# Two layers of experts on one core: the u product as one lo matmul of 256 and one hi matmul of 512 columns, a second search over 64 candidates, and three smaller edits

## The chip, the cores and the metric

The kernel runs as one program on one core of a Trainium2 chip. The metric is the time of the whole program on the device, in microseconds, as the median of the runs.

## The reference, cut to what matters

Two blocks run one after the other on 256 tokens of width 1024. Each is a mixer (S5 in block 0, NSA attention in block 1), and behind it `peer`, a search over 16384 experts:

```python
def peer(h, w_q, sub_keys, u_tab, v_tab):
    qk = (h @ w_q).reshape(b, s, H, 2, PEER_HALF)            # H = 8 heads
    sc = jnp.einsum('bshcd,hckd->bshck', qk, sub_keys)       # 128 scores per half
    s1, i1 = lax.top_k(sc[..., 0, :], K)                     # K = 16
    s2, i2 = lax.top_k(sc[..., 1, :], K)
    cand = (s1[..., :, None] + s2[..., None, :]).reshape(b, s, H, K * K)
    cidx = (i1[..., :, None] * PEER_NKEYS + i2[..., None, :]).reshape(b, s, H, K * K)
    top_s, top_pos = lax.top_k(cand, K)
    experts = jnp.take_along_axis(cidx, top_pos, axis=-1)
    gates = jax.nn.softmax(top_s, axis=-1)
    ...
        act = jax.nn.gelu(jnp.einsum('cd,ced->ce', hc, u_tab[ec])) * gc
        return jnp.einsum('ce,ced->cd', act, v_tab[ec])
```

## The kernel before

The kernel doesn't gather experts. It computes all 16384 of them for all tokens. Transposed, `B[expert, token] = gelu(u · h)`, held as 128 units of 128 experts (`NJ` = 128); then the gates, scattered to all experts, are multiplied in, and `B` times v gives the output. One `peer_layer` has these stages.

**U** (`U`, L724): for each unit j, 128 x 1024 weights are loaded (`load_unit`, L126, SP queue, `RAW` = 6 buffers shared by every load of the kernel), split into `w_hi` (an ACT copy to the short form fp32r, L139) and `w_lo` (a DVE subtraction, L181), and multiplied with h, which is split the same way into `h_hi` and `h_lo`. `mm3` (L184) issues three matmuls of 256 columns for each of the 8 slices k of the width: w_hi·h_hi (L188), w_hi·h_lo (L189), w_lo·h_hi (L190). That makes 24 matmuls a unit. Two units share one PSUM bank of 512, and `evac` takes both at once: one ACT gelu, and for the tokens that already have gates one DVE product more (L738).

**Route** (`route_steps`, L846): q for each head, scores, `topk1` (16 of 128 by MAX8, FIND_INDEX8 and MATCH_REPLACE8), `topk2` (16 of 256 sums), and `decode` (L913), which turns positions into expert numbers.

**G** (`G`, L752): 64 steps of 4 tokens. Each step writes two one-hot tables of 1024 columns on DVE (`oij` L762, `ohl` L765), multiplies them in 8 matmuls of 128 columns (L770), and multiplies the 512 results into `B` on DVE (L773), as far as the units of U are done (`ugelu`); what isn't done yet gets a copy on ACT (L776). The pool of `oij` and `ohl` has two buffers each.

**VS** (`VS`, L789): for each j, the v unit is split like u, `B[:, j]` is split into `a_hi` (ACT) and `a_lo` (DVE), and 12 matmuls of 512 columns (L799) add to four banks `acc`. In layer 0 `ada_steps` (L219) runs beside it on DVE: one load of `ada_t` and one pass of 1024 columns (L233) per step, 56 steps; DVE and SP follow the written order here.

**What sets the order.** `weave` (L698) mixes the steps of U into route and then into G by planned costs: each step yields (PE us, DVE us), and another U unit is drawn while the planned DVE time is ahead of the planned PE time. A U unit yields 2.62 for PE and `U_DVE` = 1.3 for DVE (0.6 more for each second unit once gates exist); a G step yields 0.5 and 1.5. What is left of U is drawn in VS, one unit per j, and while it lasts `credit` for ada steps grows by 0.8 per j, after that by 0.4. `peer_end` (L817) copies the four banks out (ACT L827 and DVE L825), transposes them and adds to x.

In the NSA stage `scores` (L1148) computes, for each pair of heads, head `par` = 0 from rows 0 to 63 of `qT` and `kT`, then head 1 from rows 64 to 127: a matmul of 128 columns (L1155), one of 256 (L1157), and two masks (L1159, L1160). In S5, `copies` (L568) writes `u` with the tokens of a channel in chunk order, and the matmuls of L613 read it through a strided view.

Of the kernel before, what the change touches and what calls it, by code (L numbers as in the profile page):

```python
# [282 lines left out]
class Norm:  # L283


    def __init__(self, K, g, layer, part, rs, bufs=4):
# [1130 lines left out]
```

## Time and profile before

| what | value |
|---|---|
| times of three runs | 2096.7, 2101.8, 2094.01 us |
| median | 2096.7 us |
| the profiled execution: its time, its span | 2095.41 us, 2093.6 us |
| PE busy | 2036.0 us, 97% |
| DVE busy | 1611.3 us, 77% |
| ACT busy | 1154.3 us, 55% |

By the trace S5 ends near 200 us; layer 0 of peer has its route stage to 412, G to 655 and VS to 1047; NSA ends near 1237; layer 1 of peer has decode in 1350 to 1455, G to 1690 and VS to 2080. Busy time of an engine is a sum over instructions; matmuls overlap one another, so the pace of a run of matmuls is read from their starts, not from their lengths. Idle time of an engine counts only where it is the one that others wait for.

### The profile page before, as it was taken

The numbers are of one execution on the slowest core, as the hardware profiler recorded it, in microseconds if no ns is written. First come the engines' busy times: TensorE is split into PE (matmuls) and PEld (weight loads), VectorE is DVE, ScalarE is ACT, GpSimd is POOL, SyncE is SP. The second block draws the span as 40 slices with busy tenths as digits, with TensorE's granted clock in tenths as the row PEclk, the third lists the DMA queues.
The fourth block names the chain that finished last, engine by engine and source line by source line (L and its number), as shares of the span: only waits on it lengthen the run. The fifth ranks groups of instructions, "written<-read, shape, count | busy, mean of one in ns | idle before, by whom it ended". The sixth has DMA issues, their size and how long they took to land. (4 is left out here: it accounts for less than half of the span.)

```text
span 2093.6 us, 39285 instructions
## 1 busy us (share of the span) xinstructions
PE 2036.0 (97%) x14344; PEld 1842.8 (88%) x14344; DVE 1611.3 (77%) x3698; ACT 1154.3 (55%) x2396; POOL 113.3 (5%) x149
## 2 busy tenths in 40 slices
PE   6899999999999999999999999999999999999998
PEld 3789999899999988888888689999999998888887
DVE  8696899878887777777766769998788865566555
ACT  4775555554445555555545655555454455555554
POOL 4220001200000000000010000022000000000000
PEclk9899999999999999999999999999999999999999
DMA  7445555544446788888863035555444455666663
GB/s 282 149 180 162 162 173 172 160 151 135 140 140 190 260 271 274 267 269 272 270 221 101 21 129 165 172 171 162 141 132 142 141 177 184 194 193 196 193 192 100
DMA packets 102690, 377.18 MB, mean 180 GB/s; under 512 B 11488, under 2 KB 11872, under 8 KB 101472
## 3 DMA queue, kind: packets, MB, share of 16 engines
q1 hardware_dynamic: 101520, 371.42, 55.8%
q0 software_dynamic: 544, 2.61, 0.4%
q8 instruction: 112, 1.84, 0.3%
q14 instruction: 82, 0.67, 0.1%
q10 hardware_dynamic: 432, 0.65, 0.1%
HBM read 373.07 MB, written 1.05 MB: 179 GB/s over the span
## 5 line engine op out<-in xcount | busy, mean ns | idle before, releaser
L139 ACT ACTIVATE w_hi<-raw 128x512 fp32r<-128x512 f32 x1194 | 746.8, 628 | 737.8 <-PE bank L189 433.5
L181 DVE TENSOR_TENSOR w_lo<-raw,w_hi 128x512 fp32r<-128x512 f32 x1194 | 814.9, 704 | 132.5 <-ACT w_hi L139 130.2
L188 PE MATMUL bank<-h_hi,w_hi 128*128 128x256 f32 x2504 | 717.3, 289 | 9.0 <-ACT w_hi L139 5.6
L190 PE MATMUL bank<-h_hi,w_lo 128*128 128x256 f32 x2504 | 709.1, 286 | 10.7 <-DVE w_lo L181 10.7
L189 PE MATMUL bank<-h_lo,w_hi 128*128 128x256 f32 x2504 | 709.5, 284 | 1.4 <-DVE h_lo L304 1.4
L188 PEld LDWEIGHTS bank<-h_hi,w_hi 128*128 128x128 f32 x2504 | 485.2, 195 | 17.1 <-ACT w_hi L139 7.5
L190 PEld LDWEIGHTS bank<-h_hi,w_lo 128*128 128x128 f32 x2504 | 480.2, 193 | 15.3 <-DVE w_lo L181 14.7
L189 PEld LDWEIGHTS bank<-h_lo,w_hi 128*128 128x128 f32 x2504 | 483.1, 193 | 3.8 <-DVE h_lo L304 2.7
L799 PE MATMUL bank<-w_lo,a_hi 128*128 128x512 f32 x1024 | 399.0, 390 | 0.2 <-DVE w_lo L181 0.2
L799 PE MATMUL bank<-w_hi,a_lo 128*128 128x512 f32 x1024 | 398.5, 389 | 0.0
L799 PE MATMUL bank<-w_hi,a_hi 128*128 128x512 f32 x1024 | 281.0, 390 | 0.0
L181 DVE TENSOR_TENSOR a_lo<-B,a_hi 128x256 fp32r<-128x256 f32 x256 | 108.9, 425 | 197.9 <-ACT a_hi L139 197.8
L799 PEld LDWEIGHTS bank<-w_hi,a_lo 128*128 128x128 f32 x1024 | 192.3, 188 | 39.8
L799 PEld LDWEIGHTS bank<-w_lo,a_hi 128*128 128x128 f32 x1024 | 192.3, 188 | 39.8 <-DVE w_lo L181 0.7
L799 PEld LDWEIGHTS bank<-w_hi,a_hi 128*128 128x128 f32 x1024 | 191.5, 188 | 38.6
L770 PE MATMUL bank<-ohl,oij 128*128 128x128 f16 x1024 | 129.2, 307 | 0.0
L139 ACT ACTIVATE a_hi<-B 128x256 fp32r<-128x256 f32 x256 | 106.7, 418 | 27.0 <-PE bank L799 14.4
L773 DVE SCALAR_TENSOR_TENSOR B<-bank,B 128x216 f32<-128x216 f32 (+31 forms) x128 | 62.5, 488 | 71.9 <-PE bank L770 71.1
L770 PEld LDWEIGHTS <-oij 128*128 128x128 f16 x1024 | 101.5, 128 | 4.2
L762 DVE TENSOR_TENSOR oij<-iota,slotT 128x1024 f16<-128x1024 f16 x128 | 89.2, 698 | 0.0
L765 DVE TENSOR_TENSOR ohl<-oij,slotT 128x1024 f16<-128x1024 f16 x128 | 88.8, 695 | 0.1
L233 DVE SCALAR_TENSOR_TENSOR raw<-raw,cb 128x1024 f32<-128x1024 f32 x56 | 68.3, 1219 | 0.0
(263 smaller groups left out, 1790.2 us busy)
## 6 DMA issues: line engine op xcount, KB each, us to landing
raw<-peer_u SPq DMA_DIRECT2D x256, 512.0 KB, 3.6
raw<-peer_v SPq DMA_DIRECT2D x256, 512.0 KB, 4.3
raw<-ada_t SPq DMA_DIRECT2D x56, 512.0 KB, 4.6
raw<-ada_w SPq DMA_DIRECT2D x40, 512.0 KB, 5.4
raw<-w_q SPq DMA_DIRECT2D x32, 512.0 KB, 3.5
raw<-w_glu SPq DMA_DIRECT2D x16, 512.0 KB, 4.1
raw<-w_in SPq DMA_DIRECT2D x8, 512.0 KB, 6.3
w<-w_cmp SPq DMA_DIRECT2D x4, 1024.0 KB, 9.4
```

What stands on the lines that cost most here:

```text
L139: nc.scalar.activation(hi, raw, AF.Copy)
L181: K.nc.vector.tensor_tensor(lo, raw, hi.bitcast(F32), op=OP.subtract)
L188: nc.tensor.matmul(out, wh, xh, start=start, stop=False)
L189: nc.tensor.matmul(out, wh, xl, start=False, stop=False)
L190: nc.tensor.matmul(out, wl, xh, start=False, stop=stop)
L233: V.scalar_tensor_tensor(w, w, 1.0, cb, op0=OP.mult, op1=OP.mult, accum_out=part[:, m:m + 1])
L762: V.tensor_tensor(oij.rearrange("p a n j t -> p (a n) j t"), tab[:, None].to_broadcast(full), si, op=OP.is_equal)
L765: V.tensor_tensor(ohl, oj, slotT[:, 1, 2 * q:2 * q + 2, :, None, :].to_broadcast([P, 2, 2, P, 2]), op=OP.mult)
L770: nc.tensor.matmul(pv[:, :, t], oij[:, t // 2, 0, :, t % 2], ohl[:, t // 2, n, :, t % 2], start=(n == 0), stop=(n == 1), skip_group_check= ...
L773: V.scalar_tensor_tensor(B[:, :jd, ts], pv[:, :jd], 1.0 / GS, B[:, :jd, ts], op0=OP.mult, op1=OP.mult)
L799: nc.tensor.matmul(acc[t][dh], a[al][:, ts], w[wl], start=(j == 0 and al + wl == 0), stop=(j == NJ - 1 and al == 1))
```

## The change

1. **U product.** `h_hi` and `h_lo` become halves of one tile `h2`. For each k there are now two matmuls: w_lo·h_hi of 256 columns, which opens the accumulation in the left half of a bank, and w_hi·[h_hi, h_lo] of 512 columns over the whole bank. A unit has a bank of its own. `evac` runs for each unit: ACT copies the left half to `B`, DVE adds the right half, ACT takes the gelu in place; where gates exist, the same on a tile `ge`, and then the product. A unit now yields 2.5 and `U_DVE` = 1.65 (0.3 more once gates exist). `ROUTE_J` goes from 64 to 72.
2. **Second search.** `topk2` searches 64 of the 256 sums, those that can be among the best 16 (four adds build them), and `places` turns their positions back, once per layer; the weights' exponentials of both token halves move ahead of it.
3. **Scores by turns**: the two heads' matmuls alternate, each head with its own bank.
4. **u by steps**: S5 writes `u` in the order in which L613 reads it.

```diff
-        self.hi = K.hpool.tile([P, KC, S], F32R, name="h_hi")
-        self.lo = K.hpool.tile([P, KC, S], F32R, name="h_lo")
+        K.h2 = K.hpool.tile([P, KC, 2, S], F32R, name="h2")
+        self.hi, self.lo = K.h2[:, :, 0], K.h2[:, :, 1]
...
-        u = tp.tile([P, S], F32, name="u", bufs=3)
+        u = us[k] = tp.tile([P, L, S // L], F32, name="u", bufs=3)
...
-        nc.scalar.activation(u, ps, AF.Copy)
-        us[k] = u.rearrange("p (c s) -> p s c", s=L)
+        nc.scalar.activation(u, pv, AF.Copy)
...
             def evac():
-                c, ps = late.pop()
-                pv = ps.rearrange("p (j t) -> p j t", j=2)
+                j, ps = late.pop()
                 t0 = done[0]
-                out = B[:, 2 * c:2 * c + 2]
+                out = B[:, j]
                 if t0 < S:
-                    nc.scalar.activation(out[:, :, t0:], pv[:, :, t0:], AF.Gelu_apprx_tanh)
+                    nc.scalar.activation(out[:, t0:], ps[:, t0:S], AF.Copy)
+                    V.tensor_add(out[:, t0:], out[:, t0:], ps[:, S + t0:])
+                    nc.scalar.activation(out[:, t0:], out[:, t0:], AF.Gelu_apprx_tanh)
                 if t0 > 0:
-                    g = wp.tile([P, 2, S], F32, name="ge", bufs=1)
-                    nc.scalar.activation(g[:, :, :t0], pv[:, :, :t0], AF.Gelu_apprx_tanh)
-                    V.tensor_mul(out[:, :, :t0], g[:, :, :t0], out[:, :, :t0])
-                ugelu[0] = 2 * c + 2
-                return 0.6 if t0 else 0.0
-
-            for c in range(NJ // 2):
+                    g = wp.tile([P, S], F32, name="ge")
+                    nc.scalar.activation(g[:, :t0], ps[:, :t0], AF.Copy)
+                    V.tensor_add(g[:, :t0], g[:, :t0], ps[:, S:S + t0])
+                    nc.scalar.activation(g[:, :t0], g[:, :t0], AF.Gelu_apprx_tanh)
+                    V.tensor_mul(out[:, :t0], g[:, :t0], out[:, :t0])
+                ugelu[0] = j + 1
+                return 0.3 if t0 else 0.0
+
+            for j in range(NJ):
                 ps = bank(K)
-                for m in range(2):
-                    chunk_T(K, split_w(K, load_unit(K, u_src[layer, 2 * c + m])), h, ps[:, m * S:(m + 1) * S])
-                    dve = evac() if late and m == 0 else 0.0
-                    yield 2.62, U_DVE + dve
-                late.append((c, ps))
+                w = split_w(K, load_unit(K, u_src[layer, j]))
+                for k in range(KC):
+                    hi, lo = w[k // 4]
+                    cs = slice((k % 4) * P, (k % 4 + 1) * P)
+                    nc.tensor.matmul(ps[:, :S], lo[:, cs], h[0][:, k], start=(k == 0), stop=False, skip_group_check=True)
+                    nc.tensor.matmul(ps, hi[:, cs], K.h2[:, k].rearrange("p a t -> p (a t)"), start=False,
+                                     stop=(k == KC - 1), skip_group_check=True)
+                dve = evac() if late else 0.0
+                yield 2.5, U_DVE + dve
+                late.append((j, ps))
...
-ROUTE_J = 64
-U_DVE = 1.3
+ROUTE_J = 72
+U_DVE = 1.65
+CAND = ((0, 1, 16), (1, 3, 8), (4, 4, 4), (8, 8, 1))
+NCAND = 64
...
     def topk2(u):
+        at = 0
+        for a0, na, nb in CAND:
+            shape = [P, 2, na, nb]
+            V.tensor_tensor(cand[:, :, at:at + na * nb].rearrange("p t (a b) -> p t a b", a=na),
+                            val[:, :, u, 0, a0:a0 + na, None].to_broadcast(shape),
+                            val[:, :, u, 1, None, 0:nb].to_broadcast(shape), op=OP.add)
+            at += na * nb
         for t in range(2):
-            cd = cand[t]
-            V.tensor_add(cd, val[:, t, u, 0, :, None].to_broadcast([P, 16, 16]),
-                         val[:, t, u, 1, None, :].to_broadcast([P, 16, 16]))
-            top16(ts[:, t, u], pos[:, t, u], cd.rearrange("p a b -> p (a b)"), cand2[t])
-            yield 0, 2.0
+            top16(ts[:, t, u], pos[:, t, u], cand[:, t], cand2[t])
+            yield 0, 1.4
...
     with K.tc.manual_schedule(engines={mybir.EngineType.DVE}):
+        weights()
+        yield from places()
         for t in range(2):
             yield from decode(t)
...
     def scores(i, b):
         out = []
+        gp, r = divmod(i, 4)
+        sps = [bank(K) for _ in range(2)]
+        for cs, ts, n in ((slice(P, 3 * P), slice(P, S), S), (slice(0, P), slice(0, P), P)):
+            for par in range(2):
+                rows = slice(64 * par, 64 * par + 64)
+                nc.tensor.matmul(sps[par][:, cs], qT[rows, i, ts], kT[b][rows, gp, 0:n], start=(n == S), stop=False,
+                                 skip_group_check=True)
```

**PE, one U unit of layer 0 in the route stage.** `bank` is the unit's PSUM tile. Before, the first two slices k of a unit:

```order
L188 MATMUL bank_2993<-h_hi_2662,w_hi_2996 128x256 [waits Activation_49]
L189 MATMUL bank_2993<-h_lo_2663,w_hi_2996 128x256
L190 MATMUL bank_2993<-h_hi_2662,w_lo_2997 128x256 [waits DVE_49]
L188 MATMUL bank_2993<-h_hi_2662,w_hi_2996 128x256
L189 MATMUL bank_2993<-h_lo_2663,w_hi_2996 128x256
L190 MATMUL bank_2993<-h_hi_2662,w_lo_2997 128x256
```

After, the end of one unit and the first slices of the next:

```order
L750 MATMUL bank_8146<-h2_2661,w_lo_8154 128x256
L751 MATMUL bank_8146<-h2_2661,w_hi_8153 128x512
L750 MATMUL bank_8181<-h2_2661,w_lo_8185 128x256 [waits DVE_49]
L751 MATMUL bank_8181<-h2_2661,w_hi_8184 128x512 [waits Activation_49]
L750 MATMUL bank_8181<-h2_2661,w_lo_8185 128x256
L751 MATMUL bank_8181<-h2_2661,w_hi_8184 128x512
```

Three matmuls of 256 columns per slice became one of 256 and one of 512, and the first matmul of a unit is the one that reads `w_lo`, from DVE.

**DVE, the last part of G in layer 0.** Before, one round of two G steps with the work of the U units between them; after step 64 there were still 14 U units left, which VS drew:

```order
L773 SCALAR_TENSOR_TENSOR B_2696<-bank_8306,B_2696 128x104x4 [waits PE_49]
L762 TENSOR_TENSOR oij_8405<-iota2_71,slotT_2697 128x1024 [waits DVE_49]
L181 TENSOR_TENSOR w_lo_8378<-raw_8371,w_hi_8377 128x512 [waits Activation_49]
L773 SCALAR_TENSOR_TENSOR B_2696<-bank_8321,B_2696 128x104x4 [waits PE_49]
L762 TENSOR_TENSOR oij_8420<-iota2_71,slotT_2697 128x1024 [waits DVE_49]
L765 TENSOR_TENSOR ohl_8406<-oij_8405,slotT_2697 128x1024 [waits DVE_49]
L181 TENSOR_TENSOR w_lo_8439<-raw_8436,w_hi_8438 128x512 [waits DMAHW0_49,PE_49,Activation_49]
L738 TENSOR_TENSOR B_2696<-ge_8368,B_2696 128x2x232 [waits Activation_49]
L765 TENSOR_TENSOR ohl_8421<-oij_8420,slotT_2697 128x1024 [waits DVE_49]
L181 TENSOR_TENSOR w_lo_8443<-raw_8436,w_hi_8442 128x512 [waits PE_49,Activation_49]
L181 TENSOR_TENSOR w_lo_8477<-raw_8474,w_hi_8476 128x512 [waits DMAHW1_49,PE_49,Activation_49]
```

After, the same engine: the last U unit has its product in front of G step 34, and the last 31 steps stand alone, in rounds of two steps like this one (PE has 8 pairs of LDWEIGHTS and MATMUL per step there and nothing else, then 128 V units without U):

```order
L772 TENSOR_TENSOR ohl_8381<-oij_8380,slotT_2695 128x1024 [waits DVE_49]
L772 TENSOR_TENSOR ohl_8395<-oij_8394,slotT_2695 128x1024 [waits DVE_49]
L780 SCALAR_TENSOR_TENSOR B_2694<-bank_8384,B_2694 128x128x4 [waits PE_49]
L769 TENSOR_TENSOR oij_8408<-iota2_71,slotT_2695 128x1024 [waits DVE_49]
L780 SCALAR_TENSOR_TENSOR B_2694<-bank_8398,B_2694 128x128x4 [waits PE_49]
L769 TENSOR_TENSOR oij_8422<-iota2_71,slotT_2695 128x1024 [waits DVE_49]
```

The subtractions for `w_lo` (L181) and the products L738 that stood among the G steps are gone from this part; in the first half of G some 1.8 U units are drawn per step, where it was about one.

**DVE, the end of VS in layer 0**, from the last V unit's `w_lo` to the copies of `acc`. Before:

```order
L181 TENSOR_TENSOR w_lo_12723<-raw_12716,w_hi_12722 128x512 [waits DMAHW3_49,DVE_49]
L290 SCALAR_TENSOR_TENSOR nsc_12836<-mod1_76,sm_67 128x8 [waits DVE_49]
L181 TENSOR_TENSOR w_lo_12727<-raw_12716,w_hi_12726 128x512 [waits Activation_49]
L233 SCALAR_TENSOR_TENSOR raw_12742,apart_8852<-raw_12742,cb_8849 128x1024 [waits DMAHW4_49]
L181 TENSOR_TENSOR w_lo_12887<-raw_12884,w_hi_12886 128x512 [waits DMAHW5_49,Activation_49]
L236 TENSOR_TENSOR mod1_76<-apart_8852,sm_67 128x4 [waits DVE_49]
L181 TENSOR_TENSOR w_lo_12891<-raw_12884,w_hi_12890 128x512 [waits Activation_49]
L825 COPY o_12756<-bank_8716 128x512 [waits PE_49]
```

After (`raw` in L233 is an `ada_t` load; SP issues three `peer_v` loads, then seven `ada_t` loads in a row, then `w_kc`; before it was one `ada_t` load):

```order
L181 TENSOR_TENSOR w_lo_12242<-raw_12235,w_hi_12241 128x512 [waits DMAHW5_49]
L181 TENSOR_TENSOR w_lo_12246<-raw_12235,w_hi_12245 128x512 [waits Activation_49]
L233 SCALAR_TENSOR_TENSOR raw_12261,apart_8851<-raw_12261,cb_8848 128x1024 [waits DMAHW6_49]
L233 SCALAR_TENSOR_TENSOR raw_12275,apart_8851<-raw_12275,cb_8848 128x1024 [waits DMAHW2_49,DVE_49]
L290 SCALAR_TENSOR_TENSOR nsc_12374<-mod1_76,sm_67 128x8 [waits DVE_49]
L233 SCALAR_TENSOR_TENSOR raw_12278,apart_8851<-raw_12278,cb_8848 128x1024 [waits DMAHW3_49]
L233 SCALAR_TENSOR_TENSOR raw_12281,apart_8851<-raw_12281,cb_8848 128x1024 [waits DMAHW4_49]
L832 COPY o_12294<-bank_8761 128x512 [waits PE_49]
```

Four passes of L233 now stand between the last `w_lo` of V and the first copy, where there was one.

## Rows read from the trace of the kernel before

**Rows 1.** Stretches: length; busy (count) PE, PEld, DVE, ACT, POOL; PEclk, DMA share, GB/s.

```profile
216.00:340.00 124.00, 124.00 (x1041) 124.00 (x1040) 118.08 (x465) 67.41 (x120) 0.00 (x0) 1.00 0.58 179
412.00:655.00 243.00, 243.00 (x2073) 240.89 (x2072) 195.16 (x352) 122.88 (x264) 0.00 (x0) 1.00 0.46 143
1140.00:1215.00 75.00, 75.00 (x541) 52.51 (x541) 56.10 (x241) 46.82 (x168) 0.00 (x0) 1.00 0.10 29
```

**Rows 2.** Timeline of PE, a U unit, layer 1: start, length, line, shape.

```profile
1685.95 0.28 PE L188 MATMUL bank<-h_hi,w_hi 128*128 128x256 f32 x1
...
1689.79 0.28 PE L190 MATMUL bank<-h_hi,w_lo 128*128 128x256 f32 x1
```

**Rows 3.** Chain that ended last, layer 1: start, us, line, count.

```profile
1675.06 1.76 PE bank L770 x16
...
1768.76 231.45 PE bank L799 x1021
```

**Rows 4.** Timeline of DVE, late G, layer 0; in brackets idle before.

```profile
643.62 0.61 DVE L773 SCALAR_TENSOR_TENSOR B<-bank,B 128x432 f32<-128x432 f32 x1 [1.02 <-PE bank L770]
644.14 0.68 DVE L762 TENSOR_TENSOR oij<-iota,slotT 128x1024 f16<-128x1024 f16 x1
644.74 0.69 DVE L181 TENSOR_TENSOR w_lo<-raw,w_hi 128x512 fp32r<-128x512 f32 x1
...
646.46 0.69 DVE L765 TENSOR_TENSOR ohl<-oij,slotT 128x1024 f16<-128x1024 f16 x1
```

**Rows 5.** Timeline, PE and DVE, two G steps of layer 0.

```profile
461.47 1.81 PE L770 MATMUL bank<-ohl,oij 128*128 128x128 f16 x15
...
462.56 0.41 DVE L773 SCALAR_TENSOR_TENSOR B<-bank,B 128x240 f32<-128x240 f32 x1 [1.04 <-PE bank L770]
```

**Rows 6.** Stretches of S5 where PE has gaps, columns as in rows 1.

```profile
40.00:44.00 4.00, 2.71 (x14) 0.84 (x13) 3.96 (x8) 2.10 (x5) 1.76 (x3) 1.00 1.00 406
...
48.00:52.00 4.00, 3.31 (x19) 2.90 (x19) 3.63 (x9) 1.12 (x3) 1.87 (x4) 0.81 1.02 411
96.00:100.00 4.00, 2.30 (x20) 0.82 (x19) 2.85 (x7) 3.83 (x18) 1.31 (x2) 1.00 0.01 2
100.00:104.00 4.00, 3.63 (x19) 3.43 (x20) 3.81 (x6) 3.94 (x8) 2.46 (x3) 0.71 0.12 10
```

**Rows 7.** Timeline of PE, first products of layer 0's route stage.

```profile
209.50 0.41 PE L189 MATMUL bank<-h_lo,w_hi 128*128 128x256 f32 x1
...
210.56 0.41 PE L190 MATMUL bank<-h_hi,w_lo 128*128 128x256 f32 x1
```

**Rows 8.** The page, part 5: DVE with 256 columns.

```profile
L181 DVE TENSOR_TENSOR a_lo<-B,a_hi 128x256 fp32r<-128x256 f32 x256 | 108.9, 425 | 197.9 <-ACT a_hi L139 197.8
```

**Rows 9.** Timeline of PE, NSA: a head's scores, then a pair's values.

```profile
1149.84 0.48 PE L1155 MATMUL bank<-kT,qT 64*128 64x128 f32 x2
1150.16 0.59 PE L1157 MATMUL bank<-kT,qT 64*128 64x256 f32 x2
1150.69 0.23 PE L1159 MATMUL bank<-maskb,identb 128*128 128x128 bf16 x1
...
1152.63 0.87 PE L1194 MATMUL bank<-pT,vv 128*64 128x256 f32 x8
1153.43 0.39 PE L188 MATMUL bank<-h_hi,w_hi 128*128 128x256 f32 x1
```

**Rows 10.** Timeline of PE, S5: one step of L613.

```profile
90.24 2.47 PE L613 MATMUL bank<-u,T 128*128 128x256 f32 x8
```

**Rows 11.** Waits of PE in decode, layer 0: total us, times, longest.

```profile
PE bank L190 <- DVE w_lo L181: 5.3, 7, 1.5
```

**Rows 12.** Timeline of DVE, end of VS; page, part 6, us to landing.

```profile
1043.58 1.22 DVE L233 SCALAR_TENSOR_TENSOR raw<-raw,cb 128x1024 f32<-128x1024 f32 x1
...
1046.20 0.69 DVE L825 COPY o<-bank 128x512 f32<-128x512 f32 x1
...
raw<-ada_t SPq DMA_DIRECT2D x56, 512.0 KB, 4.6
```

More of the change, by code (lines that the diff above doesn't have):

```diff
@@ L855, in route_steps @@
     sc2 = [cv([P]) for _ in range(2)]
-    cand = [cv([16, 16]) for _ in range(2)]
-    cand2 = [cv([256]) for _ in range(2)]
+    cand = cv([2, NCAND])
+    cand2 = [cv([NCAND]) for _ in range(2)]
     val = cv([2, H, 2, TK])
@@ L862, in route_steps @@
     pos = cv([2, H, TK], U32)
+    ab = cv([2, 2, H, TK])
+    assert cv.at == ROUTE_J * S + 7680
     def top16(v, i, src, tmp):
@@ new lines, in topk2, with places @@
+        for a0, na, nb in CAND:
[4 more added lines that the diff above has]
+            at += na * nb
+        for t in range(2):
+            top16(ts[:, t, u], pos[:, t, u], cand[:, t], cand2[t])
+            yield 0, 1.4
+    def places():
+        cw = Carve(B.rearrange("p j t -> p (j t)"), ROUTE_J * S + 12360)
+        sh = cw([2, 256], U32)
+        pf, m, n = cw([256]), cw([256]), cw([256])
+        f = cw([2, 256])
+        p2 = pos.rearrange("p t h k -> p (t h k)")
+        a, b = (ab[:, :, c] for c in range(2))
+        v = lambda x: x.rearrange("p (t h k) -> p t h k", t=2, h=H)
+        V.tensor_scalar(sh[:, 0], p2, 3, None, op0=OP.logical_shift_right)
+        V.tensor_scalar(sh[:, 1], p2, 2, None, op0=OP.logical_shift_right)
+        V.tensor_copy(f, sh)
+        V.tensor_copy(pf, p2)
+        V.tensor_copy(idf, idx)
+        yield 0, 1.6
+        V.tensor_scalar(m, f[:, 0], -1.0, 0.0, op0=OP.add, op1=OP.max)
+        V.scalar_tensor_tensor(m, f[:, 1], -6.0, m, op0=OP.add, op1=OP.max)
+        V.scalar_tensor_tensor(a, v(pf), -48.0, v(m), op0=OP.add, op1=OP.max)
+        yield 0, 1.2
+        V.tensor_scalar(v(m), a, 8.0, 8.0, op0=OP.mult, op1=OP.add)
+        V.scalar_tensor_tensor(v(m), a, 16.0, v(m), op0=OP.mult, op1=OP.min)
+        V.tensor_scalar(v(n), a, 4.0, 24.0, op0=OP.mult, op1=OP.add)
+        V.tensor_tensor(m, m, n, op=OP.min)
+        V.scalar_tensor_tensor(v(m), a, 48.0, v(m), op0=OP.add, op1=OP.min)
+        V.tensor_sub(b, v(pf), v(m))
+        yield 0, 2.2
@@ new lines, in route_steps, with weights @@
+    ws = []
+    def weights():
+        for t in range(2):
+            cw = Carve(B.rearrange("p j t -> p (j t)"), ROUTE_J * S + t * 7680)
+            w = dict(sel=cw([2, H, TK]), eq=cw([2, H, TK, 16]), e=cw([H, TK]), z=cw([H]), el=cw([H, TK]),
+                     e16=cw([H * TK // 2]).bitcast(F16).rearrange("p (h k) -> p h k", h=H))
+            ws.append(w)
+            V.tensor_sub(w["e"], ts[:, t], ts[:, t, :, 0:1].to_broadcast([P, H, TK]))
+            nc.scalar.activation(w["e"], w["e"], AF.Exp)
@@ L926, in decode @@
+    def decode(t):
+        sel, eq, e, z, el, e16 = (ws[t][n] for n in ("sel", "eq", "e", "z", "el", "e16"))
         shape = [P, 2, TK, 16]
@@ L930, in decode @@
                 c, hs = parts[n]
-                V.tensor_tensor(eq[:, c, hs], abf[:, c, hs, :, None].to_broadcast(shape),
+                V.tensor_tensor(eq[:, c, hs], ab[:, t, c, hs, :, None].to_broadcast(shape),
                                 K.iota[:, None, None, 0:16].to_broadcast(shape), op=OP.is_equal)
@@ L937, in decode @@
             yield 0, 1.2
-        V.tensor_sub(e, ts[:, t], ts[:, t, :, 0:1].to_broadcast([P, H, TK]))
-        nc.scalar.activation(e, e, AF.Exp)
         V.tensor_reduce(z, e, axis=AX.X, op=OP.add)
@@ L1149, in scores @@
         out = []
+        gp, r = divmod(i, 4)
[5 more added lines that the diff above has]
+                                 skip_group_check=True)
         for par in range(2):
-            gp, r = divmod(i, 4)
-            rows = slice(64 * par, 64 * par + 64)
             hd = 4 * (2 * gp + par) + r
-            sp = bank(K)
-            nc.tensor.matmul(sp[:, 0:P], qT[rows, i, 0:P], kT[b][rows, gp, 0:P], start=True, stop=False,
-                             skip_group_check=True)
-            nc.tensor.matmul(sp[:, P:3 * P], qT[rows, i, P:S], kT[b][rows, gp, :], start=False, stop=False,
-                             skip_group_check=True)
+            sp = sps[par]
             nc.tensor.matmul(sp[:, 0:P], identb, maskb, start=False, stop=True, skip_group_check=True)
```

12 lines of the change are left out of this document (removed).

## The prediction, as put on record

> **What bounds the kernel now.** I read the busy time of the stages first, then the chain that ended last, then the starts of single instructions on PE and DVE. In the stretches [rows 1] the reader sees PE busy for all 124 us of the route stage, all 243 us of G and all 75 us of the attention stretch, at the full granted clock, while DVE has 118.1, 195.2 and 56.1 us of work there. So PE sets the pace, in G because U units stand between the G steps, and DVE comes close in the route stage only. The chain in layer 1 is PE alone: two G steps of 1.76 us, later 1021 v matmuls in 231.45 us [rows 3]. What counts for the change is therefore what PE has to do, and whether PE still has something to do wherever DVE works.
>
> **U product.** Of 24 matmuls of 256 columns in a unit, the first and the last in its group start 3.84 us apart with 32 between the starts [rows 2]: 0.120 us each, 0.360 per slice, 2.88 a unit. The 512-column matmuls of VS start every 231.45/1021 = 0.2267 us [rows 3]. A slice becomes 0.120 + 0.2267 = 0.3467 us, a unit 2.77. That is 0.0133 us for each of 8 x 256 = 2048 slices: **27 us less**. The two rates differ by more than columns: 512 columns take less than twice 256, so each matmul has about 0.013 us that doesn't grow with columns. The Trainium skill (TensorE: Matmul & The Clock Gate, section "Wait — 56ns, not 53.3ns?") puts that fixed part at about 2.5 ns a matmul; by it the merge would save an estimated 5 us and the sum would end 22 us later. The rows here don't agree with it.
>
> **Evacuation per unit.** New per unit: a DVE add of 256 columns (0.425 us [rows 8]) and an ACT copy, with the gelu now in units of 256. In the part of G where U units remain, a G step on DVE is `oij` and `ohl` at 0.60 (starts 644.14 to 644.74) and the product L773 at about 0.5 [rows 4]; with 1.8 U units of two `w_lo` at 0.60, the add and a product L738 at some 0.3 that is 1.7 + 1.8 x 1.9 = 5.1 us against 0.88 + 1.8 x 2.77 = 5.9 on PE. PE covers it, so it costs nothing there. In the route stage DVE was at 118.1 of 124 [rows 1]; per head the order now has four U units instead of three, which gives PE 2.77 us more and DVE 1.2 for `w_lo` plus four adds, less what the shorter search saves. I put stalls there at 0 to 10 us, take **+3**.
>
> **U runs out in the middle of G: the largest term.** By the order shown ahead, the last U unit is used up when G step 33 is issued, and 31 steps stand alone in each layer. Before, PE's cover for those steps was U. Nothing hides DVE now. A step's 8 matmuls take 1.76/2 = 0.88 us [rows 3], and are complete 1.09 us after the first starts (461.47 to 462.56, where the waiting product begins) [rows 5]. On DVE, `oij` and `ohl` take 0.60 each, and the product 0.52 at 432 columns (643.62 to 644.14) [rows 4]; from 240 to 432 columns its length grows by 0.20 us [rows 4, 5], so at 512 it takes 0.60. The round of two steps in the new order is ohl, ohl, product, oij, product, oij. The first `ohl` is written at 0.69, PE starts at about 0.75, the first product can begin at 0.75 + 1.09 = 1.84, and four more DVE operations of 0.60 follow: the round takes 4.24 us, of which PE works 1.76. PE loses 2.48 us in 15.5 rounds: 38.5 us a layer, **77 us in both**, at the full clock. The floor is six DVE operations back to back, 3.60 us: 28.5 a layer, 57 in both.
>
> **The clock in those 31 steps.** In S5, PE was busy 2.71 of 4 us from 40 to 44 at a granted clock of 1.00, and from 48 to 52 the clock was down to 0.81; a stretch with 2.30 of 4 was followed by one at 0.71 [rows 6]. The lone G steps keep PE busy 1.76 of 4.24, which is 1.7 of 4, for 66 us on end: less than in any of these. So I expect 1.2 GHz for most of it. At 1.2 GHz the starts of 256-column matmuls lie (210.56 - 209.50)/5 = 0.212 us apart [rows 7], 1.77 times 0.120. With that factor a G step takes 1.56 us and is complete after 1.93. The second step is then complete at 0.75 + 1.56 + 1.93 = 4.24, the second product and `oij` end the round at 5.44: PE loses 5.44 - 1.76 = 3.68 us a round. Taking the first 2.5 rounds at full clock and 13 at half: 2.5 x 2.48 + 13 x 3.68 = 54 a layer, **+108 in both** (upper bound, a factor of 2: 15.5 x 4.1 = 64 a layer, 128). VS then begins at the low clock: some 4 us at half pace lose 2, and the last product, `a_hi` and `a_lo` (0.425 [rows 8]), which now have no U unit beside them, another 2: **+8** for both layers (4 if the clock never fell).
>
> **End of VS in layer 0.** Without U in VS, ada steps go at 0.4 per unit from the start, and the last ones are left over: four passes of L233 stand between the last `w_lo` and the first copy of `acc`. One pass takes 1.22 us, and the copy began at 1046.20, 2.6 us after the start of the pass ahead of it [rows 12]. The last pass needs a load whose buffer is freed by an earlier one of the four, and an `ada_t` load lands after 4.6 us [rows 12]. Last `w_lo` some 3.3 us ahead of the end of V, 1.2 for the pass that frees, about 4.6, and 1.2: the copy begins some 4 us later. **+4**, between 2 (loads early) and 7 (`w_kc` late too, behind seven loads on SP).
>
> **Decode.** PE waited 5.3 us there for `w_lo` [rows 11]; a unit now begins with the `w_lo` matmul, and DVE has the add as well as `places`. Bounds 0 to +5 a layer, take **+4** for both.
>
> **Scores by turns.** A head's scores take 0.85 us (1149.84 to 1150.69), on 64 rows; two heads 1.70, in 16 pairs. The values of a pair, the same number of matmuls with alternating halves of the output, take 0.80 (1152.63 to 1153.43) [rows 9]. If the turns work as well, 16 x 0.85 = 13.6 us go, since PE is full there [rows 1]; if the halves don't overlap, 0. Values are the nearest row; some of the softmax may show instead: **-10**. The Trainium skill (TensorEngine Tiling (Array Packing), "Key Properties") says that row tiles work independently; by it the whole 13.6 would go and the sum would end 4 us earlier. No row here has alternating row halves.
>
> **u by steps.** A step of L613 takes 2.47 us [rows 10]; its 8 matmuls have 160 columns on average, and at the pace of the contiguous scores (0.53 for two of 256 [rows 9]) it would take about 1.5. Eight steps: 0 to 7 us; S5 has gaps of its own, so **-3**.
>
> **Sum**, against the profiled execution's 2095.4 (the median of the runs is 1.3 above it, and I don't add that): 2095.4 - 27 + 3 + 108 + 8 + 4 + 4 - 10 - 3 = 2182.4, say **2182 us**.
>
> **The rivals.**
> *The clock stays at 2.4 GHz in the lone steps.* For it: gaps there are short and regular, some 2.5 us. Against it: [rows 6]. Then +77 and +4 stand in place of +108 and +8: 2147 us.
> *The evacuation holds PE.* ACT copy, DVE add and ACT gelu are a chain between two engines that serve in order, and `w_hi` and `w_lo` of the next units queue behind it; while DVE waits for a copy, `w_lo` waits, and PE for that. For it: DVE's 118.1 of 124 in the route stage [rows 1]. Against it: in G the sums above leave DVE 0.8 us of slack in 5.9. At 0.15 us for each of 256 units it is 38 us more: 2220.
> *The lone steps cost next to nothing* (the side of faster). If DVE ran ahead on the tables, and the products came so close behind that a round was bound by PE, the G term would vanish: 2182 - 108 - 8 + 0 = 2066. It decides at what the rest of the sum leaves: without the G and clock terms the change gains 29 us, over 31 rounds, so a round must take under 1.76 + 0.94 = 2.7 us. Against it: six DVE operations of 0.60 are 3.60, and there are only two buffers of each table. The same case holds if U didn't run out, which the order excludes.
> *All bounds on the good side*: 57 for the lone steps, 13.6 and 7 saved elsewhere, no stalls: 2095.4 - 27 + 57 - 13.6 - 7 + 4 = 2109, which is over 0.5% slower still; a larger gain from the merge would bring it to no change.
>
> **How the numbers follow.** Forecast 0.6, clock stays 0.2, evacuation holds PE 0.1, lone steps for nothing 0.05, the rest, near no change, 0.05. The range takes in the clock rival with its savings at the bound (2138), and above the forecast the factor of 2 and stalls of the route stage (2207). Over 0.5% is 10 us, about what a measurement can tell from no change: faster 0.05, same 0.06, slower 0.89.
>
> **What would show it.** Right: PE idle 50 us or more in the last third of G of each layer, released by DVE `ohl` and by nothing else; rounds of 4.2 to 5.5 us on DVE with products that wait for PE; a granted clock near 0.5 there; U units 2.77 us apart; copies of `acc` 4 us later in layer 0; scores of a pair in about 0.9 us. Wrong: rounds under 3 us, PE waiting in the route stage for the add or for `w_lo`, or U units still 2.88 us long.

## The result and the profile after

The changed kernel takes 2196.2 us in the median (2193.4 to 2198.9) against 2096.6: 1.0473 times the time before, 95% interval 1.0455 to 1.0491. The forecast was 2182, with a range of 2138 to 2207. The profiled execution has a span of 2193.1 us, 99.5 more than before. Its page, part 1 (busy us, share of the span, instructions):

```profile
PE 2044.5 (93%) x12296; PEld 1746.3 (80%) x12296; DVE 1682.1 (77%) x4158; ACT 1234.9 (56%) x2891; POOL 112.4 (5%) x149
```

PE has 2048 matmuls less and is still busy longer, and its share of the span is lower. Where the time is lost shows by stretches of layer 0 (length; busy PE, PEld, DVE, ACT, POOL; granted clock, DMA share, GB/s): route, decode, G with U beside it, the lone G steps.

```profile
216.00:340.00 124.00, 123.92 (x844) 114.63 (x843) 112.61 (x509) 77.44 (x161) 0.00 (x0) 1.00 0.55 182
340.00:475.00 135.00, 120.89 (x664) 100.84 (x664) 108.63 (x200) 80.86 (x174) 21.94 (x16) 1.00 0.48 160
475.00:670.00 195.00, 195.00 (x1218) 169.52 (x1217) 162.90 (x393) 130.03 (x391) 0.00 (x0) 1.00 0.49 162
671.00:747.00 76.00, 43.51 (x250) 36.84 (x248) 57.38 (x95) 4.15 (x9) 0.00 (x0) 0.73 0.00 0
```

Route and the first part of G are full; decode has 121 of 135 us, and the lone steps 43.5 of 76 at a mean clock of 0.73. Before, PE was full in all of G [rows 1]. What PE waited for in the whole run (total us, times, longest):

```profile
PE bank L777 <- DVE ohl L772: 61.9, 30, 2.4
PE bank L750 <- DVE w_lo L181: 27.8, 30, 1.7
...
PE bank L841 <- DVE o L832: 3.1, 1, 3.1
...
PE bank L806 <- ACT a_hi L139: 2.9, 2, 1.7
```

By the starts of the same instructions in both traces: S5 ends 0.6 us earlier, layer 0 of peer takes 51.5 us more (840.9 to 892.4), the NSA stage 2.6 less, layer 1 of peer 51.1 more. The NSA stage is made of two parts: from the start of the last v matmul to the norm's L279 it is 13.9 us where it was 8.05, 5.8 more, and the rest is 8.4 less.

**The lone steps.** DVE, one round of two steps in layer 0:

```profile
679.06 1.28 DVE L772 TENSOR_TENSOR ohl<-oij,slotT 128x1024 f16<-128x1024 f16 x2
680.89 0.69 DVE L780 SCALAR_TENSOR_TENSOR B<-bank,B 128x512 f32<-128x512 f32 x1 [0.54 <-PE bank L777]
681.49 0.68 DVE L769 TENSOR_TENSOR oij<-iota,slotT 128x1024 f16<-128x1024 f16 x1
682.09 0.68 DVE L780 SCALAR_TENSOR_TENSOR B<-bank,B 128x512 f32<-128x512 f32 x1
682.69 0.68 DVE L769 TENSOR_TENSOR oij<-iota,slotT 128x1024 f16<-128x1024 f16 x1
683.29 1.28 DVE L772 TENSOR_TENSOR ohl<-oij,slotT 128x1024 f16<-128x1024 f16 x2
```

From `ohl` to `ohl` it is 4.23 us: two tables, the product after a wait of 0.54 for PE, `oij`, product, `oij`, each 0.60. Two rounds later:

```profile
687.89 1.28 DVE L772 TENSOR_TENSOR ohl<-oij,slotT 128x1024 f16<-128x1024 f16 x2
690.55 0.69 DVE L780 SCALAR_TENSOR_TENSOR B<-bank,B 128x512 f32<-128x512 f32 x1 [1.38 <-PE bank L777]
```

The wait is 1.38 now, because PE does the same matmuls at half the clock. The clock by stretches of 4 us (columns as above):

```profile
676.00:680.00 4.00, 1.69 (x17) 1.41 (x16) 3.66 (x8) 0.00 (x0) 0.00 (x0) 1.00 0.00 0
680.00:684.00 4.00, 1.72 (x16) 1.44 (x14) 3.46 (x7) 0.00 (x0) 0.00 (x0) 1.00 0.00 0
684.00:688.00 4.00, 2.61 (x16) 2.13 (x16) 3.19 (x6) 0.00 (x0) 0.00 (x0) 0.64 0.00 0
688.00:692.00 4.00, 3.37 (x16) 3.12 (x16) 2.46 (x4) 0.00 (x0) 0.00 (x0) 0.51 0.00 0
692.00:696.00 4.00, 2.01 (x17) 1.87 (x16) 3.27 (x6) 0.00 (x0) 0.00 (x0) 0.92 0.00 0
```

Up to 684 the clock is at 1.00 while PE works 1.7 of 4 us. Then it falls, comes back for some microseconds, and falls again. The 31 steps last 76.0 us, from 671.1 to the first v product at 747.1, and 74.8 in layer 1 (1753.1 to 1827.9). At the pace with U beside them they would take 31 x 0.88 = 27.3. So the two stretches cost 48.7 + 47.5 = 96 us.

**The smaller places.** U slices in G, where [rows 2] had three matmuls 0.120 apart:

```profile
562.09 0.28 PE L750 MATMUL bank<-h,w_lo 128*128 128x256 f32 x1
562.20 0.40 PE L751 MATMUL bank<-h,w_hi 128*128 128x512 f32 x1
562.44 0.28 PE L750 MATMUL bank<-h,w_lo 128*128 128x256 f32 x1
...
564.52 0.28 PE L750 MATMUL bank<-h,w_lo 128*128 128x256 f32 x1
```

Seven slices take 2.43 us here, 0.347 each. Behind a G step the first interval is longer (0.20 to 0.21 instead of 0.117), so the mean over all starts is 0.355 a slice in the route stage and 0.357 in G, where before it was 0.363 and 0.367. End of VS in layer 0, the last pass of L233 and the copy on DVE, and the transposes on PE that wait 3.1 us for it (in [rows 12] the copy began at 1046.20, ahead of the end of V at 1046.9):

```profile
1099.84 1.22 DVE L233 SCALAR_TENSOR_TENSOR raw<-raw,cb 128x1024 f32<-128x1024 f32 x1
...
1100.99 0.68 DVE L832 COPY o<-bank 128x512 f32<-128x512 f32 x1
...
1101.73 2.82 PE L841 MATMUL bank<-cst,o 128*128 128x128 f32 x12 [3.08 <-DVE o L832]
```

Decode, PE's waits in layer 0, where [rows 11] has 5.3 us in 7 waits; then those of PE in both layers of the kernel before, and those of DVE's new add (L733) for ACT's copy (L732) in both layers of the changed kernel:

```profile
PE bank L750 <- DVE w_lo L181: 13.9, 15, 1.7
...
PE bank L190 <- DVE w_lo L181: 10.7, 15, 1.5
...
DVE B L733 <- ACT B L732: 46.9, 37, 2.1
```

Of the last, 23.1 us lie in decode of layer 0 (340 to 475). DVE is busy 108.6 of 135 us there: it has idle time, but it works in the written order, and what stands behind the add, `w_lo` among it, waits with it.

Attention, a pair of heads, with the first mask behind it (0.86 us, where [rows 9] has 0.85 for each head); one L612 step in S5 and the matmul behind it (1.37 us; [rows 10] has 2.47); the end of S5:

```profile
1203.41 0.92 PE L1204 MATMUL bank<-kT,qT 64*128 64x256 f32 x8
1204.27 0.23 PE L1209 MATMUL bank<-maskb,identb 128*128 128x128 bf16 x1
...
90.03 1.37 PE L612 MATMUL bank<-u,T 128*128 128x256 f32 x8
91.33 1.09 PE L617 MATMUL bank<-rH,wo 128*32 128x63 f32 x64
...
205.46 1.22 PE L279 MATMUL bank<-rs,ones 128*128 128x256 f32 x2 [1.57 <-DVE rs L277]
```

### The profile page after: what moved, and what is told of

Same layout as the page of the kernel before. It is cut to its first block, busy times and chain, and to the rows that moved or that the text cites. A ratio compares the mean times of both kernels' runs of the same rounds, so it can differ in the third digit from the quotient of the medians.

```text
span 2193.1 us, 36356 instructions
## 1 busy us (share of the span) xinstructions
PE 2044.5 (93%) x12296; PEld 1746.3 (80%) x12296; DVE 1682.1 (77%) x4158; ACT 1234.9 (56%) x2891; POOL 112.4 (5%) x149
## 4 chain that ended last, share of the span: by engine, by line
PE 59%; DVE 5%; issue 1%; ACT 0%; DMA 0%; DVEq 0%; ACTq 0%
PE bank L806 31%; PE bank L751 9%; PE bank L750 5%; PE bank L777 3%; PE bank L189 2%; PE bank L188 2%; PE bank L190 2%; DVE w_lo L181 1%; PE bank L1204 1%; PE bank L1244 1%; DVE B L780 1%; PE bank L1121 1%; DVE oij L769 1%; PE bank L1232 1%; DVE ohl L772 1%
## 5 line engine op out<-in xcount | busy, mean ns | idle before, releaser
L139 ACT ACTIVATE w_hi<-raw 128x512 fp32r<-128x512 f32 x1194 | 747.1, 628 | 603.2 <-issue 274.1
L181 DVE TENSOR_TENSOR w_lo<-raw,w_hi 128x512 fp32r<-128x512 f32 x1194 | 817.6, 709 | 104.1 <-ACT w_hi L139 100.9
L751 PE MATMUL bank<-h,w_hi 128*128 128x512 f32 x2048 | 721.0, 392 | 0.0
L750 PE MATMUL bank<-h,w_lo 128*128 128x256 f32 x2048 | 589.2, 288 | 28.2 <-DVE w_lo L181 27.8
L751 PEld LDWEIGHTS bank<-h,w_hi 128*128 128x128 f32 x2048 | 384.0, 187 | 78.0
L750 PEld LDWEIGHTS bank<-h,w_lo 128*128 128x128 f32 x2048 | 390.0, 190 | 43.6 <-issue 25.2
L181 DVE TENSOR_TENSOR a_lo<-B,a_hi 128x256 fp32r<-128x256 f32 x256 | 108.8, 425 | 220.6 <-ACT a_hi L139 220.6
L777 PE MATMUL bank<-ohl,oij 128*128 128x128 f16 x1024 | 160.7, 350 | 61.9 <-DVE ohl L772 61.9
L777 PEld LDWEIGHTS <-oij 128*128 128x128 f16 x1024 | 122.3, 145 | 89.6 <-DVE ohl L772 74.3
L188 PE MATMUL bank<-h,w_hi 128*128 128x256 f32 x456 | 132.0, 299 | 9.0 <-ACT w_hi L139 5.7
L189 PE MATMUL bank<-h,w_hi 128*128 128x256 f32 x456 | 133.5, 294 | 1.0 <-DVE h L304 1.0
L733 DVE TENSOR_TENSOR B<-B,bank 128x256 f32<-128x256 f32 (+24 forms) x256 | 97.3, 380 | 47.7 <-ACT B L732 46.9
L190 PE MATMUL bank<-h,w_lo 128*128 128x256 f32 x456 | 131.4, 293 | 1.2 <-DVE w_lo L181 1.2
L780 DVE SCALAR_TENSOR_TENSOR B<-bank,B 128x512 f32<-128x512 f32 (+22 forms) x128 | 79.7, 624 | 61.8 <-PE bank L777 61.6
L734 ACT ACTIVATE B<-B 128x256 f32<-128x256 f32 (+24 forms) x256 | 98.4, 384 | 44.3 <-DVE B L733 42.3
## 6 DMA issues: line engine op xcount, KB each, us to landing
w<-w_cmp SPq DMA_DIRECT2D x4, 1024.0 KB, 10.5
```

The costliest lines, as they stand in the source:

```text
L139: nc.scalar.activation(hi, raw, AF.Copy)
L181: K.nc.vector.tensor_tensor(lo, raw, hi.bitcast(F32), op=OP.subtract)
L188: nc.tensor.matmul(out, wh, xh, start=start, stop=False)
L189: nc.tensor.matmul(out, wh, xl, start=False, stop=False)
L190: nc.tensor.matmul(out, wl, xh, start=False, stop=stop)
L733: V.tensor_add(out[:, t0:], out[:, t0:], ps[:, S + t0:])
```

## The experiments

Theory: the loss is G steps without U beside them, on which DVE sets the pace, and the clock falls on top. Rival: the new evacuation loads DVE and ACT so that PE waits for `w_lo`, wherever the U units stand.

**Spread U over all of G.** One planning number, which moves U units only:

```diff
-                yield 2.5, U_DVE + dve
+                yield 2.5, (U_DVE if done[0] == 0 else U_G) + dve
+U_G = 1.1
```

> The changed kernel with one number more: once gates exist, a U unit is planned with 1.1 instead of 1.65 us of DVE time, so that about 0.93 U units stand beside every G step to the last one, and no G step stands alone. Theory (the loss is G steps without U beside them): the lone stretch took 75.5 us a layer where its 31 steps are 27 us of matmul time, so about 48 us a layer and 2 at the start of VS come back: 2095 to 2115 us, no wait of PE for ohl, granted clock 1.00 through G. Rival (the evacuation on DVE and ACT is the loss): with 0.93 U units per step DVE has some 3.5 us of work per step against 3.5 on PE and holds it in all 64 steps: 2130 us or more, PE waiting for w_lo through G.

Measured: 2110.7 us, 1.0064 of before (1.0047 to 1.0081). PE's waits:

```profile
PE bank L750 <- DVE w_lo L181: 27.9, 30, 1.7
...
PE bank L777 <- DVE ohl L772: 8.5, 9, 2.4
```

G of layer 0, by stretch:

```profile
475.00:705.00 230.00, 223.90 (x1467) 195.59 (x1464) 213.94 (x479) 136.10 (x420) 0.00 (x0) 1.00 0.42 138
```

The wait for `ohl` went from 61.9 to 8.5 us, the clock stays up, and 85 of the 100 us came back. So the lone steps were the greater part of the loss. But the kernel is still slower than before, and DVE is at 214 of 230 us in G: the rival has a part too, in decode (27.9 us, as in the changed kernel) and inside G (waits for `ohl` at 595, 634 and 673 us in layer 0).

**Keep PE busy in the lone steps.** Eight matmuls behind every second lone step, into a bank that nobody reads:

```diff
+                if ugelu[0] == NJ and q % 2 == FILL_AT:
+                    fill = bank(K)
+                    for n in range(FILL):
+                        nc.tensor.matmul(fill, h[0][:, n % KC, 0:P], K.h2[:, n % KC].rearrange("p a t -> p (a t)"),
+                                         start=(n == 0), stop=(n == FILL - 1), skip_group_check=True)
```

> The changed kernel with work added: after every second lone G step PE multiplies eight matmuls of 512 columns (1.8 us) into a bank that nobody reads. DVE's order and work stay. They end before the next table is there, so they can cost nothing, but keep PE busy. Theory (DVE rounds of 4.24 us, and the clock on top): the clock stays at 1.00, rounds come down to 4.24 us, and 8 to 10 us a layer and 2 at the start of VS come back: 2172 to 2180 us. If the clock cost what the prediction's two terms say (54 against 38.5 a layer): 2165. Rival (the clock costs nothing, the rounds are bound by DVE anyway): 2196 us, no change against the changed kernel.

Measured: 2173.4 us, 1.0364 (1.0347 to 1.0381): 22.8 us less than the changed kernel, though 256 matmuls were added (16 times eight in each layer). A round on DVE:

```profile
702.81 1.28 DVE L772 TENSOR_TENSOR ohl<-oij,slotT 128x1024 f16<-128x1024 f16 x2
704.63 0.69 DVE L785 SCALAR_TENSOR_TENSOR B<-bank,B 128x512 f32<-128x512 f32 x1 [0.54 <-PE bank L777]
...
707.04 1.28 DVE L772 TENSOR_TENSOR ohl<-oij,slotT 128x1024 f16<-128x1024 f16 x2
```

The lone stretch of layer 0:

```profile
672.00:745.00 73.00, 66.20 (x405) 54.28 (x404) 62.88 (x105) 7.53 (x14) 0.00 (x0) 1.00 0.07 21
```

From the second round on, rounds are 4.23 us, at a granted clock of 1.00. The clock's price is those 22.8 us, both layers and the starts of VS together. The lone stretches are 65.8 us in each layer here (670.97 to 736.78, 1742.70 to 1808.51). Over the 27.3 us of their matmuls that is 77 us in both, with the clock up: the price of DVE's rounds.

**The kernel before with lone steps.** Its own product, evacuation and search; U is drawn faster, and 21 steps a layer stand alone:

```diff
-                    yield 2.62, U_DVE + dve
+                    yield 2.62, (U_DVE if done[0] == 0 else U_G) + dve
+U_G = 1.77
```

> The kernel before with its own product, evacuation and search, and one planning number: once gates exist, a U unit is planned with 1.77 instead of 1.3 us of DVE time, so about 1.8 units are drawn per G step, U ends at step 43, 21 steps stand alone in each layer, and VS has no U. Theory (lone steps cost what they cost in the changed kernel, 48 us for 31 steps, whatever the product): 21 x 1.55 = 33 a layer, 3 at the start of VS, 4 at its end: 2165 to 2175 us. Rival (the lone steps are slow only because of the new evacuation's backlog on DVE): 2110 or less.

Measured: 2176.0 us, 1.0383 (1.0364 to 1.0403). PE's wait:

```profile
PE bank L770 <- DVE ohl L765: 41.0, 20, 2.7
```

The stretches before and after U ends in layer 0:

```profile
660.00:680.00 20.00, 20.00 (x172) 19.83 (x171) 14.57 (x24) 9.15 (x21) 0.00 (x0) 1.00 0.47 142
680.00:700.00 20.00, 11.30 (x70) 9.69 (x68) 15.46 (x25) 1.06 (x3) 0.00 (x0) 0.72 0.00 0
```

That is 80 us without any edit of the arithmetic, just over the expected 2165 to 2175. By the starts on PE the lone steps take 51.6 and 52.3 us, 33.1 and 33.8 more than 21 x 0.88, as expected; from the last v matmul to L279 it is 16.4 us, 8 more than before, where 4 were expected. So lone steps cost as much with the old product.

**w_hi first within a slice**, on top of the spread U:

```diff
-                    nc.tensor.matmul(ps[:, :S], lo[:, cs], h[0][:, k], start=(k == 0), ...)
-                    nc.tensor.matmul(ps, hi[:, cs], K.h2[:, k]..., start=False, stop=(k == KC - 1), ...)
+                    nc.tensor.matmul(ps, hi[:, cs], K.h2[:, k]..., start=(k == 0), stop=False, ...)
+                    nc.tensor.matmul(ps[:, :S], lo[:, cs], h[0][:, k], start=False, stop=(k == KC - 1), ...)
```

> As e1_spread, and in each slice the matmul of w_hi comes first and the one of w_lo second. Theory A (a unit that begins with w_lo needs it 0.24 us earlier, and decode's waits of 13.9 us a layer come from that): the waits fall to the 5 us of before, 17 us less than e1_spread in both layers. Theory B (DVE has more to do per unit in decode, and order within a slice doesn't matter): waits fall by 0.23 us each, 15 a layer, 7 us in both. Theory C (no change): equal to e1_spread.

Measured: 2102.1 us, 1.0026 (1.0016 to 1.0035), 8.7 less than the spread alone: theory B. Its waits:

```profile
PE bank L752 <- DVE w_lo L181: 20.6, 28, 1.6
...
PE bank L777 <- DVE ohl L772: 8.5, 9, 1.3
```

G of layer 0:

```profile
467.00:700.00 233.00, 228.13 (x1495) 198.93 (x1493) 217.90 (x488) 137.54 (x425) 0.00 (x0) 1.00 0.42 139
```

The order explains 7.3 us of the 17 that the waits for `w_lo` had grown. What the rest comes from, the next three show in part.

**The price of the evacuation.** Three kernels like the last one. In the first, the gelu reads the left half of the bank directly (the same is done for the tile `ge`):

```diff
-                    nc.scalar.activation(out[:, t0:], ps[:, t0:S], AF.Copy)
-                    V.tensor_add(out[:, t0:], out[:, t0:], ps[:, S + t0:])
-                    nc.scalar.activation(out[:, t0:], out[:, t0:], AF.Gelu_apprx_tanh)
+                    nc.scalar.activation(out[:, t0:], ps[:, t0:S], AF.Gelu_apprx_tanh)
```

> As e7_hifirst, but the evacuation takes the gelu of the left half alone, without the copy and the add: the product of w_hi with the low half of h is left out of the result, though PE still computes it. It shows the price of the evacuation. Theory (the add on DVE and the ACT steps around it lengthen decode and G): PE's waits for w_lo fall from 20.6 to about 10, those for ohl from 8.5 to 2, and the time to 2075 to 2085 us. Rival (they cost nothing, what e7_hifirst lacks against the sum is elsewhere on PE): 2098 to 2104.

Measured: 2059.2 us, 0.9821 (0.9806 to 0.9836), 42.9 us less than with the copy and the add. The price was expected at 17 to 27. G of layer 0:

```profile
455.00:680.00 225.00, 225.00 (x1479) 196.66 (x1477) 194.26 (x364) 112.04 (x306) 0.00 (x0) 1.00 0.43 141
```

PE waits for neither `w_lo` in U nor `ohl`, and G is 225 us long. By the starts on PE, 25 of the 43 us are saved ahead of the first G step (12.8 and 12.6 in the two layers) and 17 between it and the first v matmul (10.0 and 7.4). In the second, only the two `V.tensor_add` lines are taken out and ACT's copy stays:

> As e7_hifirst, with ACT's copy and the gelu in place, but without DVE's add: the product of w_hi with the low half of h is left out of the result, though PE computes it. Theory A (the add on DVE is the price): as e10_noadd, 2059 to 2065 us. Theory C (ACT's extra passes ahead of w_hi are the price): near e7_hifirst, 2090 to 2102.

Measured: 2057.7 us, 0.9811 (0.9795 to 0.9828). ACT's copy by itself costs nothing; what the add on DVE brings with it is the whole price, 43 to 44 us. That is two things: DVE's time (0.41 us an add), and DVE's wait for the copy, which goes with the add (39.3 us in 32 waits in e7_hifirst, none here). The third makes the sum one reduction on DVE and needs no copy:

```diff
-                    nc.scalar.activation(out[:, t0:], ps[:, t0:S], AF.Copy)
-                    V.tensor_add(out[:, t0:], out[:, t0:], ps[:, S + t0:])
+                    V.tensor_reduce(out[:, t0:], pv[:, t0:], axis=AX.X, op=OP.add)
```

> As e7_hifirst, but DVE sums both halves of the bank in one reduction over 512 elements (0.6 us by the reductions of decode), and ACT's copy is gone. Theory A (DVE's time is the price of the evacuation): DVE has 0.25 us more for each of 256 units, 10 to 30 us more than e7_hifirst, 2112 to 2132. Theory B (the price is the chain ACT copy, DVE add, ACT gelu, in which one engine waits for the other): one link less, 2080 to 2095.

Measured: 2121.6 us, 1.0120 (1.0103 to 1.0138): theory A by the time. There is a link less in the chain, 0.27 us more on DVE per unit (0.68 for 0.41), and 20 us more in all. PE's waits, and DVE's at the reduction:

```profile
PE bank L776 <- DVE ohl L771: 23.1, 14, 3.8
PE bank L751 <- DVE w_lo L181: 17.7, 27, 1.8
...
DVE B L733 <- PE bank L751: 21.7, 36, 1.5
```

The stages differ, though. By the starts in the profiled executions the loss lies in G (8.4 and 11.9 us more from the first G step to the first v matmul), and there DVE's time is the price. Ahead of G this kernel is 1 us faster in each layer, although DVE has more to do: there theory B has a share as well. How large each share is, no run here separates.

**The smaller edits, one at a time, on the kernel before.** Scores by turns alone:

> The kernel before with the scores by turns alone. Theory (the two halves of rows run beside each other, and PE is the bound there): 16 pairs save 0.84 us each, 2083 us. Prediction's value: 10 us, 2087. Rival (the softmax behind the scores shows instead): half of it or less, 2090 to 2096, with PE waiting for p in the attention stretch.

Measured: 2088.1 us, 0.9957 (0.9943 to 0.9971), 8.8 us less. By the starts on PE the score matmuls go from 27.6 to 17.1 us, 10.5 less; values and transposes beside them take 2.5 more, the masks 1.2 less. Scores with u by steps:

> The kernel before with scores by turns and u by steps, no search on 64. Against the scores alone (8.8 us less than before) it shows what u by steps gives. By the trace of the changed kernel a step of L612 takes 1.30 us instead of 2.40, but S5 ends only 0.6 us earlier: 2087.5 us. If PE were the bound in S5: 8.8 us more, 2079.

Measured: 2087.4 us, 0.9956 (0.9942 to 0.9969): 0.6 less than the scores alone, which is within the spread of the runs. Against the runs of the kernel before taken beside them, both are 8.8 us less, so u by steps shows no gain here. The second search alone:

> The kernel before with the second search over 64 alone (places and the earlier weights with it). Theory (PE is the bound in the route stage, and DVE has slack there): no change, 2092 to 2098 us. Rival A (DVE was the hidden bound of the route stage at 118 of 124 us): 5 to 10 us less. Rival B (decode's longer waits in the changed kernel come from places and the moved weights): PE's waits for w_lo rise from 10.7 toward 28 us, and 10 us more.

Measured: 2097.7 us, 1.0010 (1.0001 to 1.0019). The waits for `w_lo` fall from 10.7 to 6.1 us, and 4.1 us for `a_hi` at the start of VS appear. So the search is not what makes PE wait longer in decode of the changed kernel.

**A version that beats both**: the kernel before with the search, the scores and u by steps, and its own product.

> The kernel before with everything of the change but the u product: second search on 64, scores by turns, u by steps, all planning numbers as before. The parts alone give 8.8 us for the scores, about 0.6 for u by steps by the trace of the changed kernel, and 0 to 5 for the search: 2082 to 2088 us, faster than both kernels. If the parts hinder each other: 2090 or more.

Measured: 2086.3 us, 0.9949 (0.9936 to 0.9963). What PE waited for in U, and at the start of VS, where a G step stands directly ahead of the first v unit:

```profile
PE bank L190 <- DVE w_lo L181: 7.1, 8, 1.6
...
PE bank L798 <- ACT a_hi L139: 4.1, 2, 2.9
```

The search's planned DVE time at 1.7 instead of 1.4 puts two U units back between them:

> As e8_three, with the planned DVE time of a second search at 1.7 instead of 1.4 us, which only moves U units: the last G steps have two U units between them and the first v product, as in the kernel before, where e8_three has a G step directly ahead of it. Theory (the 4.1 us that PE waited for a_hi at the start of VS in e8_three come from that): 2080 to 2083 us, no wait for a_hi. Rival (the time goes to other waits, of decode above all): 2085 to 2087.

Measured: 2082.3 us, 0.9930 (0.9917 to 0.9942), the fastest of the kernels here that leave nothing out. There is no wait for `a_hi`, and the one for `w_lo` is

```profile
PE bank L190 <- DVE w_lo L181: 8.0, 11, 1.2
```

## Why the prediction was right, and where its terms were off

| term | predicted us | measured us | by what |
|---|---|---|---|
| u product on PE | -27 | -23 | 0.347 a slice in an unbroken row, 27 less; 4 lost again where G steps and scores break the row |
| lone steps: DVE's rounds and the last step | +81 | +77 | the lone stretches with PE kept busy |
| lone steps and start of VS: the clock | +35 | +23 | PE kept busy: 22.8 less |
| end of VS | +4 | +6 | last v matmul to L279: 13.9 against 8.05 |
| decode | +4 | +25 | late starts on PE, 20.5 a layer against 8.2; 17 of the 25 show as waits for `w_lo` |
| route stage ahead of decode | +3 | 0 | no wait of note there |
| scores by turns | -10 | -9 | alone on the kernel before |
| u by steps | -3 | -1 | end of S5; no gain in the pair of runs |
| sum | +87 | +98 | span: +99.5 |

The late starts are what the intervals between two starts on PE in U have over the usual ones (0.117 behind a matmul of 256 columns and 0.230 behind one of 512; before, 0.120). The rows of waits show less, since they count from a matmul's modelled end: in the changed kernel the interval from 430.29 to 430.65 is no wait there, and the one from 431.93 to 432.88 is one of 0.55.

**Right.** The largest term came from the order alone, as 31 steps a layer without cover. The round was forecast at 4.24 us and is 4.23, and the 81 us of the rounds and the last step at full clock came out as 77. That the clock falls in it was read from S5 [rows 6], and it fell.

**Partly luck.** That the total lies only 14 us from the forecast is luck in part: the sum took some 30 us too little, most of it in decode, and some 20 too much, most of it for the clock.

**Signs.** Of the signs that were put down, several came: rounds of 4.23 to 5.50 us on DVE, a pair's scores in 0.86 us, and the first copy of `acc` some 4 us later against the end of V. Some failed. PE is idle 32.5 us in the lone stretch of layer 0 (43.5 of 76.0 busy, part of it at half the clock), not 50 or more; the mean clock there is 0.73, not near 0.5. And a sign of being wrong came: PE waits for `w_lo` in decode, which is part of the route stage.

**The clock's size.** I took half clock from the third round to the end. It alternates: the mean over the stretch is 0.73, not about 0.5. The direction of that step was right, its size half too large (35 for 23); the rival in which the clock stays up fell.

**Decode is the step that failed most**, 25 for 4 and outside its bounds of 0 to 5 a layer. I put down the add in DVE's order, but took its cost as if nothing stood behind it. With the add gone all waits for `w_lo` in U go. What the trace shows is the chain that I had as a rival: DVE stands 23.1 us in decode of layer 0 at the add until ACT's copy is there, and `w_lo` stands behind it. Decode also has more U units: from 340 us to the first G step 41 in layer 0, where it was 21. One more thing counts on DVE there, a `w_lo` that starts while POOL works, and POOL's pass:

```profile
428.82 1.77 DVE L181 TENSOR_TENSOR w_lo<-raw,w_hi 128x512 fp32r<-128x512 f32 x1
...
428.38 1.66 POOL L982 TENSOR_TENSOR B<-B 128x512 f32<-128x512 f32 x1 [1.69 <-DVE B L980]
```

It takes 1.77 us instead of 0.69 [rows 4] and ends at 430.59, 0.55 behind the pass (430.04). In each of the 16 passes in decode of layer 0 one `w_lo` starts like this and ends 0.54 to 0.55 us behind the pass, 13 us of DVE in all. The kernel before has POOL's passes too, with the same 0.55, so this isn't new. How much of the waits it causes stays open; no run here takes POOL's passes away.

**The rival on the evacuation** had a chance of 0.1 and 38 us. Its mechanism is there: what the add brings costs 43 us once U is spread, 25 ahead of G and 17 in G. The changed kernel pays the part in decode. The part in G doesn't show in it, since U units stand in the first half of G in such number that PE is the bound there (no wait in 475 to 670). The lone steps and this price have one root: DVE's work in G is more than before, and planning 1.65 for a unit moved it behind U rather than away. I costed the add at nothing in G, with PE's 5.9 us against 5.1, by looking at the first half alone.

**The u product.** Its step used the two rates of [rows 2, 3], and in an unbroken row they hold: 0.347 a slice. The step left out the breaks. Behind each G step the first interval is 0.20 to 0.21 instead of 0.117, and over the slices of the route stage (216 to 340 us) and of G, intervals longer than usual add up to 1.8 and 4.75 us a layer, where it was 1.1 and 3.7. So it is 23 rather than 27. The fixed part of about 2.5 ns a matmul that the Trainium skill gives (TensorE: Matmul & The Clock Gate, section "Wait — 56ns, not 53.3ns?") would make it an estimated 5 us. The trace doesn't agree: one matmul less saves 13 ns a slice here.

**u by steps** brought three of the eight steps from 2.40 to 1.30 us on PE and all eight from 19.9 to 16.4, but S5 ends only 0.6 us earlier: PE isn't the bound in S5.

## What to carry to other kernels

A filler with a planned price is a budget for the whole stage. Where a unit's planned DVE time is raised, count how many units are left at the stage's end: a table of costs can move a gap in the cover to another place, but it doesn't fill it. A product that costs PE less but needs one more pass on a busy engine beside it can lose more there than it gains: here 23 us on PE against 43 for the add on DVE, which without it has 194 of 225 us of work in G. Ask not only whether that engine has time, but what stands behind the new pass in its order while it waits. Undo such a change in its parts before giving it up: three of the four parts, with one planning number moved, were worth 14 us.
